# Scheduler priorities for weight loads, weight splits and accumulator readers in a two-layer decoder step

## The chip, the cores and the metric

The kernel runs on one core of one Trainium2 chip. The metric is device time in microseconds for one launch; the time before is the median of three runs, 2555.13 us (2554.44 to 2561.5).

## The reference

One inference step of a two-layer decoder over a prompt of 1024 tokens and 8 single-token samples that share all weights; model width 1024, feed-forward width 2816, all in float32.

```python
hn = rmsnorm(h, g[0])
mix = a_mixer(hn, ...) if l < N_A else b_mixer(hn, ...)   # one layer of each
h = h + rmsnorm(mix, g[1])
h = h + rmsnorm(swiglu(rmsnorm(h, g[2]), w_gu[l], w_down[l]), g[3])
# swiglu(x) = (silu(x @ gate) * (x @ up)) @ w_down
```

Mixer A is a gated linear recurrence (4 heads, a 128 x 128 state per head) beside cross-attention into 256 memory tokens. Mixer B is stick-breaking attention over one shared key and value projection, beside the same kind of memory attention. For the 8 samples the shared keys and values come from a paged cache and the memory keys and values from a cache of their own.

## The kernel before

**Tiling.** The tokens are cut into two groups: group 0 has 512 prompt tokens, group 1 has 512 prompt tokens and the 8 samples (520 columns, done as two matmuls of 260). Activations lie feature by token. Float32 precision is made from fast matmuls: each operand is split into a rounded part and a remainder, and three products are summed (line 261). An activation is split by `split_to` (lines 270 to 272).

**A projection.** `proj` (lines 256 to 268) makes 128 output features: eight 128-row blocks of the weight, three products each, so 24 matmuls of 512 columns for group 0 and 48 of 260 for group 1, all summed in one accumulator tile `mm` (two such tiles exist, line 62). Its weight comes from `split_w` (lines 240 to 254), in two tiles of 4 blocks: SyncE issues the load of 256 KB into `raw` (tag `w`, 5 buffers, line 51), ScalarE makes the rounded part (line 250), VectorE the remainder (line 251), both in a `ws` tile (5 buffers, line 52). The buffers of both tags thus hold two and a half projections of eight blocks. `mem_values` (lines 598 to 618) uses the same two tags without `split_w`.

**Readers of the accumulators.** In the feed-forward block (class `ffn`, line 459, method `part`) the gate's accumulator is read by VectorE in `silu` (line 281), the up projection's by the multiplication at line 474, and the down projection's by `evac_raw` (lines 397 to 405): a ScalarE copy for the first part (line 401), a VectorE addition to the sum `r` after that (line 403). `silu` is also used by mixer A's query and gate projections, and `evac_raw` by the output projection (line 420).

**What sets the order.** The main function (lines 1143 to 1195) emits the stages and interleaves them by hand: `weave` takes turns between an attention or recurrence stage and the projections of another group. The framework then builds each engine's queue when the program is compiled: it steps through the program on its own clock, and whenever an engine is free it takes, of the instructions whose inputs and buffers are ready by that clock, the one with the lowest priority number, which is the order of emission. On the chip each engine runs its queue in that fixed order and waits on semaphores. The stages named below are the start (`start`, lines 329 to 366, which loads the tokens, squares them at line 322 and transposes them at line 352), the recurrence's sample step (`hgrn_sample`, line 816, with one-column matmuls at line 849), stick-breaking attention over the prompt (`sb_prompt`, lines 1032 to 1078, with the sums through line 1063 and the values at line 1075), and the attention of the samples (`sample_scores` and `sample_pv`, lines 671 to 714, with VectorE work of 1024 elements a partition at lines 690, 691 and 702).

Of the kernel before, what the change touches and what calls it, by code (L numbers as in the profile page):

```python
# [8 lines left out]
F32 = mybir.dt.float32  # L9
F32R = mybir.dt.float32r  # L10
# [3 lines left out]
ALU = mybir.AluOpType  # L14
# [3 lines left out]
P = 128  # L18
# [4 lines left out]
def tile_decoder(  # L23
# [6 lines left out]
    nc = tc.nc  # L30
# [16 lines left out]
    def pool(name, bufs, **kw):  # L47
        return ctx.enter_context(tc.tile_pool(name=name, bufs=bufs, **kw))

    const = pool("const", 1)  # L50
    wraw = pool("wraw", 5)
    wspl = pool("wspl", 5)
# [15 lines left out]
    def nm(s):  # L68
        uid[0] += 1
        return f"{s}_{uid[0]}"  # L70

    def T(dt=F32):
        return tpool.tile([P, WID], dt, tag="t", name=nm("t"))
# [13 lines left out]
    def M(dt=F32):  # L87
        return mpool.tile([P, 2, WID], dt, tag="m", name=nm("m"))
# [4 lines left out]
    def R_one():  # L93
        r = rpool.tile([P, ND, WID], F32, tag="r", name=nm("r"))
        return [r[:, k, :] for k in range(ND)]
# [11 lines left out]
    def small(shape, dt=F32, tag="sm", bufs=None):  # L107
        return spool.tile(shape, dt, tag=tag, name=nm(tag), bufs=bufs)
# [39 lines left out]
    for lv in range(7):  # L148
        m = 1 << lv
# [17 lines left out]
    def gcol(l, i, k):  # L167
        o = (l * 4 + i) * ND + k
        return par[:, o : o + 1]
# [64 lines left out]
    def pv(ps, g):  # L234
        return ps[:, 0, :G] if g == 0 else ps[:, :, : PW[1]]

    def sv(ap, g):
        return ap[:, :G] if g == 0 else ap.rearrange("p (a n) -> p a n", a=2)

    def split_w(W, k0, nk, m0):  # L240
        out = []
        for a in range(0, nk, 4):
            n = min(4, nk - a)
            raw = wraw.tile([P, 4, P], F32, tag="w", name=nm("w"))
            nc.sync.dma_start(
                raw[:, :n, :],
                W[(k0 + a) * P : (k0 + a + n) * P, m0 : m0 + P].rearrange("(k p) m -> p k m", p=P),
            )
            ws = wspl.tile([P, 2, 4, P], F32R, tag="ws", name=nm("ws"))
            nc.scalar.copy(ws[:, 0, :n, :], raw[:, :n, :])  # L250
            nc.vector.tensor_sub(ws[:, 1, :n, :], raw[:, :n, :], ws[:, 0, :n, :].bitcast(F32))  # L251
            for i in range(n):
                out.append((ws[:, 0, i, :], ws[:, 1, i, :]))
        return out

    def proj(g, W, k0, nk, m0, xt):
        w = split_w(W, k0, nk, m0)
        ps = mmp.tile([P, 2, 512], F32, tag="mm", name=nm("mm"))
        for k in range(nk):
            wh, wl = w[k]  # L260
            for wi, (wt, xi) in enumerate(((wh, 0), (wh, 1), (wl, 0))):
                for a in range(NPC[g]):
                    o = a * PW[g]
                    nc.tensor.matmul(  # L264
                        ps[:, a, : PW[g]], wt, xt[k][:, xi, o : o + PW[g]],
                        start=(k == 0 and wi == 0), stop=(k == nk - 1 and wi == 2),
                    )
        return ps

    def split_to(dst, src):  # L270
        nc.scalar.copy(dst[0], src)  # L271
        nc.vector.tensor_sub(dst[1], src, dst[0].bitcast(F32))  # L272

    def silu(dst, ps, g):


        n = NG[g]
        x = T()
        dst = T() if dst is None else dst
        d = dst[:, :n]  # L280
        nc.vector.tensor_scalar(sv(x, g), pv(ps, g), -44.0, None, op0=ALU.max)  # L281
        nc.scalar.activation(d, x[:, :n], AF.Exp, scale=-1.0)  # L282
        nc.scalar.activation(d, d, AF.Ln, bias=1.0)  # L283
        nc.scalar.activation(d, d, AF.Exp, scale=-1.0)  # L284
        nc.vector.tensor_mul(d, d, x[:, :n])  # L285
        return dst
# [11 lines left out]
    def sq_acc(acc, src, k, n):  # L298
        if k == 0:
            nc.scalar.activation(acc[:, :n], src, AF.Square)  # L300
        else:
            t = N()
            nc.scalar.activation(t[:, :n], src, AF.Square)  # L303
            nc.vector.tensor_add(acc[:, :n], acc[:, :n], t[:, :n])  # L304
# [92 lines left out]
    def evac_raw(g, R, ps, m, acc, first, last):  # L397
        n = NG[g]
        dst = sv(R[m], g)
        if first:  # L400
            nc.scalar.copy(dst, pv(ps, g))
        else:
            nc.vector.tensor_add(dst, dst, pv(ps, g))  # L403
        if last:
            sq_acc(acc, R[m][:, :n], m, n)

    class out_proj:
# [5 lines left out]
        def mm(self, xo, m0=0, m1=ND):  # L413
            g = self.g
            if m0 == 0:
                self.R = R_from(self.store)
                self.acc = small([P, WID], tag="st", bufs=3)
            for m in range(m0, m1):
                ps = proj(g, w_o[self.l], 0, ND, m * P, xo)
                evac_raw(g, self.R, ps, m, self.acc, True, True)  # L420
                yield
# [37 lines left out]
    class ffn:  # L459
# [4 lines left out]
        def part(self, pi):  # L464
            g, l = self.g, self.l
            n = NG[g]
            f0, nf = PARTS[pi]
            last = pi == len(PARTS) - 1
            mids = []
            for j in range(nf):  # L470
                pg = proj(g, w_gu[l], 0, ND, (f0 + j) * P, self.xt)
                sg = silu(None, pg, g)
                pu = proj(g, w_gu[l], 0, ND, DFF + (f0 + j) * P, self.xt)
                nc.vector.tensor_mul(sv(sg, g), sv(sg, g), pv(pu, g))  # L474
                mt = M(F32R)
                split_to((mt[:, 0, :n], mt[:, 1, :n]), sg[:, :n])
                mids.append(mt)
                yield
            if pi == 0:
                self.R = R_one()  # L480
            if last:
                self.acc = small([P, WID], tag="st", bufs=3)
            for m in range(ND):
                ps = proj(g, w_down[l], f0, nf, m * P, mids)
                evac_raw(g, self.R, ps, m, self.acc, pi == 0, last)
                if last and self.rows:
                    nc.scalar.activation(
                        self.R[m][:, :n], self.R[m][:, :n], AF.Copy, scale=gcol(l, 3, m)
                    )
                    if m == 3:  # L490
                        self.first_half()
                if m % 2:
                    yield
# [79 lines left out]
    def mem_keys(l):  # L573
        for h in range(H):
            w = split_w(w_mem_kv[l], 0, ND, h * P)
            pb = mmp.tile([P, 2, 512], F32, tag="mm", name=nm("mm"))
            ps, pt = pb[:, 0, :], pb[:, 1, :]
            for k in range(ND):
                wh, wl = w[k]
                for wi, (wt, xi) in enumerate(((wh, 0), (wh, 1), (wl, 0))):  # L580
                    nc.tensor.matmul(
                        ps[:, :NM], wt, memt[k // 2][:, xi, k % 2, :],
                        start=(k == 0 and wi == 0), stop=(k == ND - 1 and wi == 2),
                    )
            src = T()
            nc.scalar.copy(src[:, :NM], ps[:, :NM])
            nc.sync.dma_start(mks[l][:, h, :], src[:, :NM])
            for tb in range(2):
                nc.tensor.transpose(pt[:, tb * P : (tb + 1) * P], src[:, tb * P : (tb + 1) * P], ident)
            tok = T()  # L590
            nc.vector.tensor_copy(tok[:, :NM], pt[:, :NM])
            nc.sync.dma_start(
                mk_prompt[l, 0, :, h, :].rearrange("(t p) d -> p t d", p=P),
                tok[:, :NM].rearrange("p (t d) -> p t d", t=2),
            )
            yield
# [349 lines left out]
    class mixer_a:  # L946
# [6 lines left out]
        def fq(self):  # L953
            yield from gate_proj(self.g, self.W, self.xt, self.F, self.K)
            yield from heads2(self.g, self.W, 0, self.xt, silu, A, self.Q)
# [16 lines left out]
        def gate(self):  # L972
            yield from heads2(self.g, self.W, 12 * P, self.xt, silu, A, self.sg)
# [254 lines left out]
```

## Time and profile before

| | us |
|---|---|
| median of 3 runs (lowest, highest) | 2555.13 (2554.44, 2561.5) |
| profiled execution: its own time | 2559.18 |
| profiled execution: span of its instructions | 2557.5 |
| granted TensorE clock over the span | 0.992 |

The profile page is that of one execution. The busy time of an engine is the union of its instructions; matmuls overlap and their ends are modelled, so TensorE counts as busy when it runs slowly too. "PE" is TensorE's matmuls, "PEld" its weight loads, "DVE" VectorE, "ACT" ScalarE, "SPq" SyncE's queue, which issues nearly all DMAs. In a row of groups the numbers after the bar are busy us, mean ns of one, and the idle time before them with what ended it. A row of waits gives microseconds in total, times, and the longest. A row of stretches gives length, busy time of each engine with its count of instructions, the granted clock, and the DMA share and rate.

### The profile page before, as it was taken

How to read it: one execution, taken by the hardware profiler on the slowest of the kernel's cores; microseconds unless marked ns; L12 is line 12 of the kernel's file. 1: busy time of each engine (PE TensorE's matmuls, PEld its weight loads, DVE VectorE, ACT ScalarE, POOL GpSimd, SP SyncE). 2: the span in 40 equal slices, each digit the busy share in tenths (PEclk: the TensorE clock that was granted, in tenths of full speed). 3: DMA queues.
4: the chain of work that ended last, by engine and by line, in shares of the span. 5: the costliest groups of instructions: out<-in, count | busy, mean ns of one | idle time of the engine just before them, and what ended most of it. 6: DMA issues, size and time to landing. Idle time of an engine off the chain costs nothing.

```text
span 2557.5 us, 40523 instructions
## 1 busy us (share of the span) xinstructions
PE 2526.6 (99%) x15649; PEld 2205.3 (86%) x15649; DVE 1555.5 (61%) x2709; ACT 1183.6 (46%) x2186; POOL 40.7 (2%) x59
## 2 busy tenths in 40 slices
PE   8999999999999999999999999999999999999998
PEld 6888898888867888999999989867776798999998
DVE  6666566654675576555544576666678758444445
ACT  6346543243434455555433454566543245443334
POOL 1000000000000000000000000000021000000000
PEclk9999999998999999999999999999999999999999
DMA  6352242233563445322333446322157544333332
GB/s 183 110 161 71 73 150 77 65 111 110 158 182 91 128 153 178 103 86 60 97 94 92 125 146 189 113 82 75 46 175 217 156 125 125 111 88 100 95 92 67
DMA packets 457708, 297.91 MB, mean 116 GB/s; under 512 B 17573, under 2 KB 422642, under 8 KB 457514
## 3 DMA queue, kind: packets, MB, share of 16 engines
q1 hardware_dynamic: 454954, 286.92, 37.4%
q0 software_dynamic: 2560, 8.39, 1.1%
q8 instruction: 123, 2.02, 0.3%
q14 instruction: 71, 0.58, 0.1%
HBM read 265.44 MB, written 29.80 MB: 115 GB/s over the span
## 4 chain that ended last, share of the span: by engine, by line
issue 25%; PE 22%; DVE 1%; POOL 1%; DMA 1%; ACT 0%; DVEq 0%; POOLq 0%; SPq 0%; ACTq 0%
PE mm L264 21%; POOL c L731 1%; PE s L704 0%; DMA w<-in_w_gu 0%; DMA b<-qd 0%; DMA c<-in_cache_sb_v,pidx 0%; PE s L1125 0%; DVE c L690 0%; DVE sc L691 0%; PE ns L293 0%; PE s L440 0%; DVE yT L542 0%; DVE c L702 0%; PE s L508 0%; DVE yT L539 0%
## 5 line engine op out<-in xcount | busy, mean ns | idle before, releaser
L264 PE MATMUL mm<-x,ws 128*128 128x260 f32 (+1 forms) x10080 | 1676.5, 324 | 6.0 <-DVE ws L251 3.1
L264 PEld LDWEIGHTS mm<-x,ws 128*128 128x128 f32 x10080 | 1452.6, 189 | 167.4 <-issue 24.6
L250 ACT CAST ws<-w 128x512 fp32r<-128x512 f32 (+1 forms) x800 | 475.6, 595 | 911.9 <-PE mm L264 816.7
L251 DVE TENSOR_TENSOR ws<-w,ws 128x512 fp32r<-128x512 f32 (+1 forms) x800 | 522.2, 658 | 346.6 <-ACT ws L250 336.7
L264 PE MATMUL mm<-m,ws 128*128 128x260 f32 (+1 forms) x3168 | 542.6, 325 | 1.1 <-DVE t L474 0.5
L264 PEld LDWEIGHTS mm<-m,ws 128*128 128x128 f32 x3168 | 453.4, 188 | 59.8 <-issue 15.3
L403 DVE TENSOR_TENSOR r<-r,mm 128x520 f32<-128x520 f32 (+1 forms) x128 | 88.3, 690 | 88.9 <-PE mm L264 87.8
L281 DVE TENSOR_SCALAR t<-mm 128x512 f32<-128x512 f32 (+1 forms) x104 | 72.2, 694 | 110.2 <-PE mm L264 109.0
L474 DVE TENSOR_TENSOR t<-t,mm 128x512 f32<-128x512 f32 (+1 forms) x88 | 60.8, 691 | 116.1 <-PE mm L264 116.0
L285 DVE TENSOR_TENSOR t<-t,t 128x512 f32<-128x512 f32 (+1 forms) x88 | 61.1, 695 | 84.9 <-ACT t L284 84.8
L304 DVE TENSOR_TENSOR st<-st,n 128x512 f32<-128x512 f32 (+1 forms) x98 | 67.1, 691 | 6.9 <-ACT n L303 5.0
L272 DVE TENSOR_TENSOR m<-t,m 128x512 fp32r<-128x512 f32 (+1 forms) x88 | 61.0, 693 | 3.5 <-ACT m L271 1.6
L282 ACT ACTIVATE t<-t 128x512 f32<-128x512 f32 (+1 forms) x88 | 55.9, 635 | 12.1 <-DVE t L281 4.6
L271 ACT CAST m<-t 128x512 fp32r<-128x512 f32 (+1 forms) x88 | 54.9, 623 | 13.9 <-DVE t L474 6.9
L283 ACT ACTIVATE t<-t 128x512 f32<-128x512 f32 (+1 forms) x88 | 55.9, 635 | 2.6
L284 ACT ACTIVATE t<-t 128x512 f32<-128x512 f32 (+1 forms) x88 | 55.9, 635 | 2.3
L892 PEld LDWEIGHTS s<-a,a 128*128 128x128 f32 x448 | 53.4, 192 | 1.2
L892 PE MATMUL s<-a,a 128*128 128x64 f32 x448 | 53.1, 271 | 0.0
L731 POOL DMA_INDIRECT c<-in_cache_sb_k,pidx x16 | 16.6, 1038 | 1874.7 <-DVE r L403 1247.9
L1027 DVE SCALAR_TENSOR_TENSOR b<-b,b 128x512 f32<-128x512 f32 (+3 forms) x48 | 26.8, 558 | 29.7 <-ACT b L1026 29.3
L643 ACT ACTIVATE b<-s,nmx 128x256 f32<-128x256 f32 x64 | 29.8, 470 | 28.7 <-DVE nmx L637 28.7
L1075 PE MATMUL s<-b,a 128*128 128x512 f32 (+3 forms) x96 | 41.5, 514 | 0.3
(293 smaller groups left out, 1948.0 us busy)
## 6 DMA issues: line engine op xcount, KB each, us to landing
w<-in_w_gu SPq DMA_DIRECT2D x352, 256.0 KB
w<-in_w_down SPq DMA_DIRECT2D x160, 256.0 KB
w<-in_w_in_a SPq DMA_DIRECT2D x80, 256.0 KB
w<-in_w_o SPq DMA_DIRECT2D x64, 256.0 KB
w<-in_w_mem_kv SPq DMA_DIRECT2D x32, 256.0 KB
c<-in_cache_mem_k SPq DMA_DIRECT2D x16, 512.0 KB
c<-in_cache_mem_v SPq DMA_DIRECT2D x16, 512.0 KB
w<-in_w_kv SPq DMA_DIRECT2D x32, 256.0 KB
```

Source lines behind the costliest of these rows:

```text
L250: nc.scalar.copy(ws[:, 0, :n, :], raw[:, :n, :])
L251: nc.vector.tensor_sub(ws[:, 1, :n, :], raw[:, :n, :], ws[:, 0, :n, :].bitcast(F32))
L264: nc.tensor.matmul(ps[:, a, : PW[g]], wt, xt[k][:, xi, o : o + PW[g]], start=(k == 0 and wi == 0), stop=(k == nk - 1 and wi == 2),)
L272: nc.vector.tensor_sub(dst[1], src, dst[0].bitcast(F32))
L281: nc.vector.tensor_scalar(sv(x, g), pv(ps, g), -44.0, None, op0=ALU.max)
L282: nc.scalar.activation(d, x[:, :n], AF.Exp, scale=-1.0)
L283: nc.scalar.activation(d, d, AF.Ln, bias=1.0)
L285: nc.vector.tensor_mul(d, d, x[:, :n])
L304: nc.vector.tensor_add(acc[:, :n], acc[:, :n], t[:, :n])
L403: nc.vector.tensor_add(dst, dst, pv(ps, g))
L474: nc.vector.tensor_mul(sv(sg, g), sv(sg, g), pv(pu, g))
L892: nc.tensor.matmul(plv[:, hh, c, :], K_[:, hh, cs], rhs, start=True, stop=True)
```

## The change

Three places are put under `tc.high_priority(offset=N)`, which lowers the priority number of the instructions in the block by N, as if they had been emitted N instructions earlier. The arithmetic, tiles, buffers and the sequence of emission stay the same.

```diff
     def split_w(W, k0, nk, m0):
         out = []
-        for a in range(0, nk, 4):
+        with tc.high_priority(offset=400):
+            for a in range(0, nk, 4):
...             # load, cast and remainder as before, one level deeper
     def silu(dst, ps, g):
...
-        nc.vector.tensor_scalar(sv(x, g), pv(ps, g), -44.0, None, op0=ALU.max)
+        with tc.high_priority(offset=100):
+            nc.vector.tensor_scalar(sv(x, g), pv(ps, g), -44.0, None, op0=ALU.max)
     def evac_raw(g, R, ps, m, acc, first, last):
...
+        with tc.high_priority(offset=100):
+            if first:
+                nc.scalar.copy(dst, pv(ps, g))
+            else:
+                nc.vector.tensor_add(dst, dst, pv(ps, g))
     # ffn.part
...
-                nc.vector.tensor_mul(sv(sg, g), sv(sg, g), pv(pu, g))
+                with tc.high_priority(offset=100):
+                    nc.vector.tensor_mul(sv(sg, g), sv(sg, g), pv(pu, g))
```

More of the change, by code (lines that the diff above doesn't have):

```diff
@@ L241, in split_w @@
         out = []
-        for a in range(0, nk, 4):
[L243 to L253, printed above, removed]
+        with tc.high_priority(offset=400):
+            for a in range(0, nk, 4):
+                n = min(4, nk - a)
+                raw = wraw.tile([P, 4, P], F32, tag="w", name=nm("w"))
+                nc.sync.dma_start(
+                    raw[:, :n, :],
+                    W[(k0 + a) * P : (k0 + a + n) * P, m0 : m0 + P].rearrange("(k p) m -> p k m", p=P),
+                )
+                ws = wspl.tile([P, 2, 4, P], F32R, tag="ws", name=nm("ws"))
+                nc.scalar.copy(ws[:, 0, :n, :], raw[:, :n, :])
+                nc.vector.tensor_sub(ws[:, 1, :n, :], raw[:, :n, :], ws[:, 0, :n, :].bitcast(F32))
+                for i in range(n):
+                    out.append((ws[:, 0, i, :], ws[:, 1, i, :]))
         return out
@@ L399, in evac_raw @@
         dst = sv(R[m], g)
[L400 to L403, printed above, removed]
+        with tc.high_priority(offset=100):
[3 more added lines that the diff above has]
+                nc.vector.tensor_add(dst, dst, pv(ps, g))
         if last:
```

## The prediction

> **What bounds the kernel.** I read the page first: the span and the engines' busy time.
>
> ```profile
> span 2557.5 us, 40523 instructions
> ...
> PE 2526.6 (99%) x15649; PEld 2205.3 (86%) x15649; DVE 1555.5 (61%) x2709; ACT 1183.6 (46%) x2186; POOL 40.7 (2%) x59
> ```
>
> TensorE is busy for all but 30.9 us of the span, and the change takes no matmul away. What can be won is therefore that idle time and time in which TensorE runs below its clock. Next, the page's groups for the instructions that are moved, and the waits of ScalarE and of SyncE's queue in front of them:
>
> ```profile
> L264 PE MATMUL mm<-x,ws 128*128 128x260 f32 (+1 forms) x10080 | 1676.5, 324 | 6.0 <-DVE ws L251 3.1
> ...
> L250 ACT CAST ws<-w 128x512 fp32r<-128x512 f32 (+1 forms) x800 | 475.6, 595 | 911.9 <-PE mm L264 816.7
> L251 DVE TENSOR_TENSOR ws<-w,ws 128x512 fp32r<-128x512 f32 (+1 forms) x800 | 522.2, 658 | 346.6 <-ACT ws L250 336.7
> ```
>
> ```profile
> SPq L245 <- DVE ws L251: 1643.8, 692, 13.3
> ```
>
> ```profile
> ACT ws L250 <- PE mm L264: 816.7, 502, 7.4
> ```
>
> There are 800 loads, 800 casts and 800 remainders. Before 692 of the loads SyncE stood waiting for a remainder to give a raw buffer back, and before 502 of the casts ScalarE stood waiting for TensorE to give a `ws` buffer back. There the weights are as early as five buffers allow, and a lower priority number cannot bring them earlier. It can act only where a load, cast or remainder had its buffer and stood behind other work. To find that place I took the stretches in which TensorE is not full:
>
> ```profile
> 0.00:21.00 21.00, 10.98 (x34) 7.50 (x35) 11.41 (x32) 13.00 (x28) 7.29 (x27) 1.00 0.80 234
> ...
> 700.00:720.00 20.00, 18.59 (x79) 13.85 (x77) 18.76 (x26) 4.34 (x10) 0.00 (x0) 1.00 0.75 213
> 720.00:740.00 20.00, 18.97 (x75) 12.55 (x74) 18.22 (x25) 5.79 (x10) 0.00 (x0) 1.00 0.67 195
> 1900.00:1920.00 20.00, 18.18 (x72) 14.27 (x71) 18.66 (x25) 6.73 (x11) 8.69 (x10) 0.91 0.79 224
> ...
> 1980.00:2000.00 20.00, 16.97 (x67) 13.65 (x68) 16.45 (x22) 6.14 (x10) 0.00 (x0) 0.91 0.74 222
> 1880.00:2040.00 160.00, 153.94 (x637) 112.02 (x636) 131.40 (x185) 52.26 (x97) 27.95 (x27) 0.98 0.66 201
> ...
> 2120.00:2500.00 380.00, 379.94 (x3041) 372.04 (x3041) 194.37 (x301) 158.58 (x268) 0.00 (x0) 1.00 0.34 101
> ```
>
> The start has 10.0 us of idle TensorE, 700 to 740 has 2.4, 1880 to 2040 has 6.1. A pure feed-forward stretch (2120 to 2500) is full to 0.06 us: nothing is to be won there. The middle two are the stages where the samples' attention runs beside the feed-forward block, and there VectorE is the crowded engine (18.76 of 20 us, 18.66 of 20). The groups of those stretches name what TensorE waited for, first 1895 to 1990, then 700 to 730:
>
> ```profile
> L264 PE MATMUL mm<-x,ws 128*128 128x512 f32 x234 | 57.7, 407 | 5.1 <-DVE ws L251 3.1 <-DVE t L474 1.8 <-ACT ws L250 0.3
> ```
>
> ```profile
> L264 PE MATMUL mm<-m,ws 128*128 128x512 f32 x96 | 23.7, 399 | 1.1 <-DVE t L474 0.5 <-DVE r L403 0.4 <-DVE ws L251 0.2
> ```
>
> All of it is remainders, casts and accumulator readers, the instructions that the change moves forward. The worst place in order of time:
>
> ```profile
> 1979.54 1.22 DVE L691 TENSOR_REDUCE sc<-c 128x8 f32<-128x1024 f32 x1
> 1980.67 0.68 DVE L474 TENSOR_TENSOR t<-t,mm 128x512 f32<-128x512 f32 x1
> ...
> 1981.26 1.22 DVE L691 TENSOR_REDUCE sc<-c 128x8 f32<-128x1024 f32 x1
> ...
> 1982.39 0.68 DVE L272 TENSOR_TENSOR m<-t,m 128x512 fp32r<-128x512 f32 x1
> 1982.99 2.49 DVE L251 TENSOR_TENSOR ws<-w,ws 128x512 fp32r<-128x512 f32 x4
> ```
>
> Four remainders ran in one go at 1982.99, behind sample reductions of 1.22 us; TensorE had nothing to multiply.
>
> **The change, part by part.** No instruction is added or removed; each term is a wait that goes or comes.
>
> *Remainders, casts and readers in the sample stages.* With the change they stand ahead of lines 690, 691 and 702 whenever both are ready; what runs already is finished first (at most 1.22 us), and the second accumulator and the `ws` buffers cover that. I take the whole of 5.1 + 1.1 = 6.2 us as gone. Bounds: 0, if the queues come out in another unlucky order, and 6.2.
>
> *The clock after those waits.* The granted clock fell right behind the wait above:
>
> ```profile
> 1983.70:1986.00 2.30, 2.27 (x5) 1.82 (x6) 2.30 (x4) 0.00 (x0) 0.00 (x0) 0.50 0.76 230
> ```
>
> The two 20 us stretches at 0.91 lost 2 x 20 x 0.09 = 3.6 us of full-speed work. If the waits go, this goes: -3.6 (bounds -3.6 and 0). [...]
>
> *What the samples pay.* Their VectorE work is now last in line. 1880 to 2040 leaves VectorE 28.6 of 160 us idle, which can hold it; the output projection that follows needs their result. Bounds 0 and 6.2 (all that was won is waited for again); I take +2.0, near the wait that exists already:
>
> ```profile
> PE s L704 <- DVE c L703: 1.9, 2, 1.0
> ```
>
> *The start.* The first projection is emitted well within 400 instructions of the program's beginning, so its five loads now have the lowest numbers of all and need nothing but free buffers. Before, in order of time:
>
> ```profile
> 0.79 0.40 SPq L120 DMA_DIRECT2D xtok<-in_x_prompt  x1
> 1.25 0.57 SPq L114 DMA_DIRECT2D prow<-in_g_norm  x1
> ...
> 3.03 1.30 SPq L120 DMA_DIRECT2D xtok<-in_x_prompt  x3
> ...
> 4.70 1.06 ACT L322 ACTIVATE c<-xtok 128x1024 f32<-128x1024 f32 x1 [2.63 <-DMA xtok<-in_x_prompt]
> ...
> 9.12 1.04 ACT L322 ACTIVATE c<-xtok 128x1024 f32<-128x1024 f32 x1
> ...
> 10.72 1.04 ACT L322 ACTIVATE c<-xtok 128x1024 f32<-128x1024 f32 x1
> ...
> 15.19 0.80 PE L264 MATMUL mm<-x,ws 128*128 128x512 f32 x1 [0.81 <-ACT x L355]
> ```
>
> Five weight issues (about 0.4 us each, as the token's 0.40) and the four small ones from 1.25 to 3.03 come before the first token load: it is issued at 0.79 + 2.0 + 1.8 = 4.6 instead of 0.79, so the first squares begin near 8.4 instead of 4.70. At their own pace of 1.6 us (9.12 to 10.72) the fourth begins at 8.4 + 4.8 = 13.2, 2.5 later; the weights' casts, now done by then, give a few tenths back. I take +2.2. Bounds: -0.8 (nothing is late and the wait of 0.8 at 15.19 goes) and +5.6 (1.31 MB of weights go through first at the 234 GB/s of the first 21 us).
>
> *Everywhere else* (attention over the prompt, normalisations): within 2.5 projections the order shifts by one or two instructions of 0.6 to 0.7 us; I take 0, with the slower rival's price as the bound above.
>
> Sum: -6.2 - 3.6 + 2.0 + 2.2 = **-5.6 us**. The profiled execution took 2559.18 (1.7 us outside its span of 2557.5) and would take 2553.6. It is 4.05 above the median, so the forecast on the median is 2555.13 - 5.6 = **2549.5 us**.
>
> **Rivals.**
>
> *More is won* (2541.5). The clock is down elsewhere too, beside the one-column matmuls of the recurrence's sample step:
>
> ```profile
> 560.00:567.00 7.00, 7.00 (x23) 5.79 (x22) 1.39 (x2) 0.62 (x1) 0.00 (x0) 0.52 0.50 147
> ...
> 584.00:591.00 7.00, 7.00 (x23) 5.74 (x22) 0.69 (x1) 0.62 (x1) 0.00 (x0) 0.52 0.44 144
> ...
> 611.00:622.00 11.00, 11.00 (x56) 11.00 (x56) 1.34 (x3) 0.49 (x2) 0.00 (x0) 0.53 0.42 128
> ```
>
> That cost 7 x 0.48 x 2 + 11 x 0.47 = 11.9 us. If ready weights let the queue put dense products between the thin ones, half of it goes (-6), and the samples' 2.0 is not paid: 2549.5 - 8.0 = 2541.5. Against it: TensorE was not waiting there (11.00 of 11 busy), so weights were no obstacle.
>
> *The change does little* (2557). The counts of 692 and 502 speak for it: the buffers set the pace, the waits in the sample stages come back in another form, and only the start's 2.2 is felt.
>
> *Slower, by stick-breaking attention* (2568). A block's two accumulations at line 1063 wait for a cast and a subtraction on ScalarE and VectorE:
>
> ```profile
> L1063 PE MATMUL s<-b,trir 128*128 128x512 f32 (+3 forms) x96 | 38.9, 408 | 1.4 <-ACT b L271 0.8
> ```
>
> ```profile
> PEld s L1063 <- ACT b L271: 10.3, 34, 0.7
> ```
>
> Of 96 blocks, 34 already see their weight load wait 0.30 us. If a weight's cast (0.60) or remainder (0.66) now stands in front of that cast on the chip, TensorE, whose order is fixed, waits with the feed-forward's products behind it. If the other 62 wait as long, that is +18.6: 2568. It ends slower by over 0.3% once it eats 13.3 us, some 44 of the 62. [...] Against the rival: the queue is built with such delays in view, and only 1.4 us of idle TensorE stand before these 96.
>
> **How the numbers follow.** Forecast 0.43, with a range of its own from 2543 to 2556; more won 0.19; little 0.15; slower 0.23. About 0.3% (7.7 us) is what a measurement of this kernel can tell from no change: faster is below 2547.5, slower above 2562.8. A third of the forecast's case (0.14) and the first rival make faster 0.33; the slower rival nearly alone makes slower 0.22; the rest is 0.45. The range reaches from 2536, just past the first rival, to the slower rival's 2568, where about half of that case is left out.
>
> **What would show it.** Right: no idle before line 264 by lines 251, 474 and 403 in the two sample stages, a granted clock of 1.00 there, weight loads first in SyncE's queue and the first product of line 264 near 17.4 us. Wrong: waits of line 264 for lines 251 or 474 as long as before (the first term); the first product at 15 us (the start); waits at lines 704 or at the output projection's first products over 5 us (the samples); more idle before lines 1063 and 1075 (the last rival); or a clock below 1.00 in stretches where it is full now.

## The result and the profile after

| | before | after |
|---|---|---|
| median us (lowest, highest; runs) | 2557.58 (2553.58, 2563.02; 7) | 2568.92 (2565.26, 2571.46; 7) |
| ratio of the two, 95% interval | | 1.0049 [1.0038, 1.0061] |
| profiled execution, span | 2557.5 | 2567.2 |
| granted clock over that span | 0.992 | 0.995 |

The changed kernel is 0.49% slower where 0.2% faster was forecast, and ends 0.9 us above the range. The lines of the kernel stand 1 to 4 further down: line 251 is now 252 (remainder), 264 is 265 (product), 474 is 478, 1063 is 1067. The page of the changed kernel, the span, the engines and the two rows of products (from the tokens `x`, and from the feed-forward's inner product `m`):

```profile
span 2567.2 us, 40625 instructions
...
PE 2521.9 (98%) x15649; PEld 2198.1 (86%) x15649; DVE 1560.0 (61%) x2706; ACT 1186.4 (46%) x2189; POOL 50.6 (2%) x59
...
L265 PE MATMUL mm<-x,ws 128*128 128x260 f32 (+1 forms) x10080 | 1668.0, 323 | 2.9 <-DVE x L273 1.5
...
L265 PE MATMUL mm<-m,ws 128*128 128x260 f32 (+1 forms) x3168 | 544.6, 326 | 4.3 <-DVE t L478 2.0
```

The second of these rows before:

```profile
L264 PE MATMUL mm<-m,ws 128*128 128x260 f32 (+1 forms) x3168 | 542.6, 325 | 1.1 <-DVE t L474 0.5
```

TensorE is busy for 4.7 us less (2521.9 instead of 2526.6) in a span that is 9.7 longer: it is idle for 45.3 us instead of 30.9, 14.4 more. The first row's idle time fell from 6.0 to 2.9, but the second's rose from 1.1 to 4.3, so the products wait for 7.2 us where they waited for 7.1. What they wait for has changed: the waits for remainders (3.3 us in all) are gone, those for accumulator readers only fell from 2.6 to 2.0 (line 478, once), and 4.8 us for splits of tokens and of `m` are new. The rest of the new idle time is elsewhere.

To place it I summed TensorE's matmul work along each trace (each matmul counted by its shape) and asked at which time both traces had done the same amount. The difference of the two times is the lag of the changed kernel; only the stretches where it moved are listed:

```text
stretch (us, before)              lag gained   lag then
start, to the first products           +9.1       +9.1
76 to 138                              +1.5      +10.2
586 to 655, recurrence sample step     -5.5       +4.1
717 to 784, first sample stage         -1.4       +2.5
913 to 975, first key/value proj.      +3.3       +6.6
1484 to 1546, second key/value proj.   +3.9      +10.6
1889 to 2090, second sample stage      -1.1       +9.8
all others (each within 0.8)           -          +10.0 at the end
```

Two kinds of place lose: the start, and the two places where a normalisation feeds the key and value projection. The timeline of the changed kernel's first 25 us, to be laid beside that of before:

```profile
0.79 9.99 SPq L246 DMA_DIRECT2D w<-in_w_in_a  x10
...
10.83 0.57 SPq L114 DMA_DIRECT2D prow<-in_g_norm  x1
...
12.61 1.78 SPq L120 DMA_DIRECT2D xtok<-in_x_prompt  x4
...
14.51 0.45 PE L164 MATMUL s<-ident,prow 128*128 128x128 f32 x1 [14.51 <-DMA prow<-in_hg_lb]
...
16.20 1.06 ACT L324 ACTIVATE c<-xtok 128x1024 f32<-128x1024 f32 x1 [0.51 <-DMA xtok<-in_x_prompt]
...
21.08 1.04 ACT L324 ACTIVATE c<-xtok 128x1024 f32<-128x1024 f32 x1
...
24.90 1.22 PE L265 MATMUL mm<-x,ws 128*128 128x512 f32 x2
```

Ten weight loads, not five, stand ahead of everything in SyncE's queue, and they hold it for 9.99 us. The first token load is issued at 12.61 instead of 0.79, the first square runs at 16.20 instead of 4.70, the first product at 24.90 instead of 15.19. What held the queue is in SyncE's waits over the first 13 us:

```profile
SPq L246 <- DVE ws L252: 3.6, 4, 1.3
SPq L246 <- DMA w<-in_w_in_a: 1.2, 2, 0.7
...
SPq L246 <- DVE cmpr L135: 0.7, 1, 0.7
```

There are five raw buffers. Loads six to ten wait for VectorE to give one back: four waits are named after a remainder, and one after the small mask instruction that ran just behind the fifth remainder. The tokens' load stands behind them in the same queue. The row of loads ends at ten because only five remainders run ahead of the first product: their five `ws` buffers come back behind products. At the normalisations, the stretches of 50 us with the two key/value projections (length, busy PE, PEld, DVE, ACT, POOL with counts, clock, DMA share, GB/s), of before and then of after:

```profile
900.00:950.00 50.00, 49.96 (x335) 44.91 (x335) 43.12 (x69) 27.85 (x49) 0.00 (x0) 1.00 0.49 151
...
1500.00:1550.00 50.00, 49.90 (x371) 46.63 (x372) 32.10 (x54) 20.65 (x37) 0.00 (x0) 1.00 0.46 140
```

```profile
900.00:950.00 50.00, 48.00 (x333) 42.80 (x332) 43.83 (x69) 27.67 (x48) 0.00 (x0) 1.00 0.41 129
...
1500.00:1550.00 50.00, 46.69 (x313) 41.65 (x313) 34.41 (x57) 22.19 (x39) 0.00 (x0) 1.00 0.44 133
```

TensorE was full there before (0.04 and 0.10 us idle), and now misses 2.0 and 3.3 us; what it waits for are the splits of the normalised tokens and the copies behind the first products (the groups of 1500 to 1550, after):

```profile
L265 PE MATMUL mm<-x,ws 128*128 128x260 f32 (+1 forms) x293 | 45.1, 310 | 2.0 <-DVE x L273 1.0 <-ACT x L272 1.0
L1008 PE MATMUL s<-ident,t 128*128 128x128 f32 x16 | 2.6, 283 | 1.2 <-ACT t L1003 1.2
```

### The profile page after: what moved, and what is told of

Read it like the earlier page. It is cut to its first block, busy times and chain, and to the rows that moved or that the text cites. A ratio compares the mean times of both kernels' runs of the same rounds, so it can differ in the third digit from the quotient of the medians.

```text
span 2567.2 us, 40625 instructions
## 1 busy us (share of the span) xinstructions
PE 2521.9 (98%) x15649; PEld 2198.1 (86%) x15649; DVE 1560.0 (61%) x2706; ACT 1186.4 (46%) x2189; POOL 50.6 (2%) x59
## 4 chain that ended last, share of the span: by engine, by line
PE 67%; issue 26%; DVE 3%; ACT 2%; DMA 1%; POOL 1%; SPq 0%; DVEq 0%; POOLq 0%; ACTq 0%
PE mm L265 56%; PE s L896 2%; POOL c L735 1%; PE s L667 1%; PE mm L612 1%; PE mm L585 1%; PE s L636 1%; PE s L708 1%; DVE ws L252 1%; PE s L660 1%; PE s L1067 0%; PE s L1079 0%; ACT ws L251 0%; PE ns L295 0%; PE s L923 0%
## 5 line engine op out<-in xcount | busy, mean ns | idle before, releaser
L735 POOL DMA_INDIRECT c<-in_cache_sb_k,pidx x16 | 23.1, 1445 | 1878.2 <-DVE r L406 1244.3
```

## The experiments

Each was run in up to 12 executions beside the kernel before on the same chip. One thing has to be separated first. Executions of one and the same kernel spread over some 10 us, and the spread follows the granted clock of the execution: of the 24 runs of the kernel before that stand beside head_spared, the spans at a clock of 0.991 and 0.992 are 2559.2 to 2560.2, those at 0.995 and 0.996 are 2550.3 to 2552.4. A thousandth of clock over 2556 us is 2.6 us; a line fitted over the 186 executions of this table, each taken from the mean of its own kernel and chip, gives 2.3. The last two columns split each difference of the means that way: what the mean clock explains (at 2.6), and the rest, which is work that came later or earlier. The standard error of a difference of means is about 1 us (1.7 for held_sample), so a rest below 1 can't be told from none.

| kernel | ratio to before [95%] | mean clock, this and before | by the clock, us | the rest, us |
|---|---|---|---|---|
| head_spared | 1.0011 [1.0002, 1.0020] | 0.9949, 0.9937 | -3.1 | +5.1 |
| five_first | 1.0030 [1.0018, 1.0042] | 0.9932, 0.9937 | +1.4 | +5.9 |
| ten_first | 1.0049 [1.0036, 1.0062] | 0.9938, 0.9937 | -0.2 | +12.3 |
| readers_only | 0.9996 [0.9986, 1.0007] | 0.9939, 0.9937 | -0.5 | -0.2 |
| norm_first | 1.0021 [1.0010, 1.0031] | 0.9952, 0.9940 | -3.3 | +9.2 |
| norm_alone | 1.0034 [1.0021, 1.0048] | 0.9935, 0.9940 | +1.2 | +7.2 |
| sample_alone | 0.9985 [0.9975, 0.9994] | 0.9953, 0.9940 | -3.3 | -0.7 |
| sample_readers | 0.9966 [0.9954, 0.9979] | 0.9955, 0.9940 | -3.9 | -4.3 |
| held_norm | 0.9999 [0.9989, 1.0008] | 0.9934, 0.9932 | -0.4 | +0.4 |
| held_only | 0.9995 [0.9986, 1.0004] | 0.9933, 0.9932 | -0.1 | -0.8 |
| held_head | 0.9979 [0.9970, 0.9988] | 0.9953, 0.9932 | -5.3 | +0.3 |
| held_sample | 0.9957 [0.9944, 0.9970] | 0.9952, 0.9932 | -5.0 | -3.8 |

**The start.** Theory: the weight loads ahead of the tokens cost about 9 us. Three kernels: the change without weights ahead of the first projection's own place (the offset grows from 0 to 400 as the program goes on), and the kernel before with only the first five, and only the first ten, weight tiles moved.

```diff
 # head_spared, on the changed kernel; wp[0] is the last weight tile's place
-        with tc.high_priority(offset=400):
+        with tc.high_priority(offset=woff()):   # max(0, min(400, p - wp[0] - 10))
 # five_first (5) and ten_first (10), on the kernel before
+            with tc.high_priority(offset=400 if wn[0] <= 5 else 0):
```

> The changed kernel, with the weights' offset cut at the start so that no weight comes ahead of the first projection's place; from there it grows with the distance to 400. Theory A (the start): the first product of the projections came at 24.90 us instead of 15.19, and this is the loss. Then the first product is back at 15 to 16 us, and the time falls by 9 to 10, to within 3 us of the kernel before (2557.6). Theory B (crowding: casts and remainders stand in front of other work on ScalarE and VectorE, as the prediction's slower rival had it): the time stays at 2564 or more.

> The kernel before, with only the first five weight tiles (load, cast, remainder) 400 ahead; nothing else is moved. The prediction's arithmetic for the start (five loads ahead of the tokens) gives +2.2 to 2.5 us and the first product near 17.5. Theory A, that it was ten loads, says the same of five. The rival, that the weights' bytes and not the order of issue delay the tokens, says +5.6 and a first product near 21.

> The kernel before, with only the first ten weight tiles 400 ahead. Theory A (five more loads wait for the first five remainders and hold SyncE's queue until then): first token load issued near 12.6 us, first product near 25, +9 to 10 us in all. Theory B: +2 to 6, since the rest of the kernel is as before.

head_spared's median is 2559.11 against 2556.68, and its first product runs at 15.35; the lag at the start is +0.2 instead of +9.1. ten_first alone has +8.8 at the start, its first token load goes out at 12.01 and its first product runs at 24.75, and its median is 2568.05: the loss of the start comes from ten tiles. With five, the lag at the start is +4.9. The timeline of five_first:

```profile
0.79 2.65 SPq L249 DMA_DIRECT2D w<-in_w_in_a  x5
...
5.42 3.30 SPq L120 DMA_DIRECT2D xtok<-in_x_prompt  x4
...
12.10 0.20 ACT L180 ACTIVATE lbt<-lbt 128x4 f32<-128x4 f32 x1 [2.38 <-DVE lbt L179]
12.21 1.04 ACT L326 ACTIVATE c<-xtok 128x1024 f32<-128x1024 f32 x1
...
20.80 1.22 PE L268 MATMUL mm<-x,ws 128*128 128x512 f32 x2
```

The issues took 2.65 us for five (0.53 each) and the tokens' load went out at 5.42, near the 4.6 of the prediction. But the first square ran at 12.21 instead of the 8.4 of the prediction. Its last visible wait is no transfer: a small exponential (line 180) stands in front of it on ScalarE and waits 2.38 us for VectorE, which was busy with weight remainders (the last at 9.05) and with masks. When the tokens were there can't be read from this trace. The first product at 20.80 and the +4.9 are near the rival's numbers (21 and +5.6, by the weights' bytes), not near those of the prediction's arithmetic. The DMA engines were busy for 0.98 of 3.5 to 8 us and 0.90 of 8 to 12, so bytes can't be ruled out. Of the five tiles' cost the issues are some 0.5 us each; how much of the rest is bytes and how much is the queue order on ScalarE and VectorE stays open.

**The readers.** The kernel before with lines 281, 401, 403 and 474 100 ahead and no weight moved.

```diff
 # readers_only, on the changed kernel
-        with tc.high_priority(offset=400):
+        with tc.high_priority(offset=0):
```

> The changed kernel with the weights' offset set to 0: only the accumulators' readers are 100 ahead. Theory A: the start is as before (first product at 15.2) and the time is within 4 us of before; the waits at the two normalisations near 940 and 1530 us (3.3 and 3.9 us later in the changed kernel) do not appear, because they are the casts' doing. Theory B with the readers as its cause: these waits are there, +5 to 7 us.

2556.16 against 2556.68, ratio 0.9996 [0.9986, 1.0007]: by themselves the readers change nothing that can be measured, and the lag has no step at the normalisations. Both losses belong to the weights.

**The normalisations.** First, are the steps the weights' doing in that place? norm_alone moves weights only from the first product of the output projection to the end of each key/value projection. norm_first takes head_spared and puts the scalings and splits of `normed`, and the copies of line 999 behind the key/value products, 500 ahead of their place, so that weights no longer pass them.

```diff
 # norm_alone, on the kernel before: offset 400 between these lines, else 0
+    OFF[0] = 400
     drain(o1.mm(a1.xo, 0, 1))
...
     drain(kv_proj(0, xk0))
+    OFF[0] = 0
 # norm_first, on head_spared (normed)
+            with tc.high_priority(offset=500):
                 t = N() if keep else R[k]
```

> The kernel before, with the weights 400 ahead only in the two stretches from the first product of the output projection up to the end of the key and value projection; readers not moved. Theory A: +7 us, in two steps of 3 to 4 us near 940 and 1530 us; TensorE waits there for the normalisation's split (lines 271, 272) and for line 999. Rival (the steps need the other moves too): within 2 us of before.

> The changed kernel with the start spared as in head_spared, and with two more things 500 ahead: the normalisation's own scaling and split (lines 310 to 312 of the kernel before) and the copy that reads the key and value projection's accumulator (line 999). Theory A (at the two normalisations, near 940 and 1530 us, casts of weights that still wait for a buffer stand in front of this work on ScalarE): the two steps of 3.3 and 3.9 us go, and the time is 6 to 7 us below head_spared, near 2552.5, faster than before by 0.1 to 0.2%. Rival (it is the order on TensorE itself, in which two projections are interleaved as their inputs arrive, that costs the time): the steps stay, 2559.

norm_alone has the two steps, +3.2 and +4.5, and is slower by 0.34%. norm_first did not take them away (+4.0 and +3.3, and some +1.7 more behind the first). That speaks against the theory that weights' casts pass the normalisation's own work on ScalarE, but doesn't settle it, since this edit moved other work too, as comes out below. What VectorE did while the key/value projection waited told more. The groups on VectorE from the first scaling of this normalisation to the last split, in the kernel before (922.6 to 938.9), then in norm_alone (913.8 to 932.5):

```profile
L310 DVE SCALAR_TENSOR_TENSOR n<-r,par,st 128x512 f32<-128x512 f32 x8 | 5.8, 746 | 1.5 <-ACT st L295 1.4
L272 DVE TENSOR_TENSOR x<-n,x 128x512 fp32r<-128x512 f32 x8 | 5.3, 684 | 0.0
L251 DVE TENSOR_TENSOR ws<-w,ws 128x512 fp32r<-128x512 f32 x5 | 3.4, 684 | 0.0
L310 DVE SCALAR_TENSOR_TENSOR r<-r,par,st 128x512 f32<-128x512 f32 x3 | 2.2, 747 | 0.0
```

```profile
L325 DVE SCALAR_TENSOR_TENSOR n<-r,par,st 128x512 f32<-128x512 f32 x8 | 5.8, 746 | 1.5 <-ACT st L310 1.5
L286 DVE TENSOR_TENSOR x<-n,x 128x512 fp32r<-128x512 f32 x8 | 5.3, 684 | 0.0
L325 DVE SCALAR_TENSOR_TENSOR r<-r,par,st 128x512 f32<-128x512 f32 x7 | 5.1, 747 | 0.0
L265 DVE TENSOR_TENSOR ws<-w,ws 128x512 fp32r<-128x512 f32 x5 | 3.4, 684 | 0.0
```

The remainders are five in both. What is new is the row `r<-r`: seven instead of three. These are the scalings of the *second* normalisation of the same sum (`xb0`, emitted after the key/value projection, so with a far higher priority number). No priority holds them back: whenever VectorE has nothing else ready by the clock of the framework's scheduler, they are taken, and in the fixed queue they then stand in front of a split that comes ready a moment later. In the changed kernel, in order of time:

```profile
942.55 1.41 DVE L312 SCALAR_TENSOR_TENSOR r<-r,par,st 128x512 f32<-128x512 f32 x2
942.66 0.62 ACT L272 CAST x<-n 128x512 fp32r<-128x512 f32 x1 [1.85 <-DVE n L312]
943.88 0.68 DVE L273 TENSOR_TENSOR x<-n,x 128x512 fp32r<-128x512 f32 x1
```

The cast that the last split needs is done at 943.28; the split itself starts at 943.88, behind two scalings. That there are more such moments with the weights moved is read from the counts; why the scheduler sees more of them isn't shown. norm_first put these scalings 500 ahead too, since both normalisations use the same lines, and had eight of them in front.

Theory "scalings" against rival "weights" (the rounding and the remainders themselves make the chain late) was tested by making the second normalisation depend on the last split of the first, with eight VectorE instructions on one column each. The values don't change (gain plus 0 times a remainder).

```diff
 # held_norm on norm_alone, held_only on the kernel before,
 # held_head on head_spared, held_sample on sample_readers
+    gs0 = after_split(xk0, 1, 0)       # gg[:, k] = 0 * last split + gcol(1, 0, k)
     drain(kv_proj(0, xk0))
-    weave((normed(0, f0.R, f0.r, lambda k: gcol(1, 0, k), xb0), 8), ...
+    weave((normed(0, f0.R, f0.r, gs0, xb0), 8), ...
```

> norm_alone (the kernel before, weights 400 ahead only from the first output projection to the end of each key/value projection), with the second normalisation's scalings made to depend on the last split of the first: its eight gain columns are copied into a small tile (gain + 0 x that remainder), eight tiny VectorE instructions. Nothing is left out. Theory 'scalings': in norm_alone 7 or 8 in-place scalings of the second normalisation (0.74 us each) stand on VectorE among the 8 scalings and splits that the key/value projection waits for, against 3 before; held back, the stretch from first residual sum to last split falls from 44 us to 41 or less, PE's idle time there to under 0.5, both steps of the drift (+3.2, +4.5) go to under 1, and the time is within 0.1% of before (ratio 0.999 to 1.001). Rival 'weights': the rounding and remainders themselves, taken earlier, make the chain late; the steps stay at +2 to +4 each and the ratio at 1.002 to 1.0035.

> The kernel before, only with the second normalisation's scalings held back as in held_norm; no priority is moved. Both theories: PE's idle time in the two normalisations was 0.0 and 0.07 us before, so nothing can be won there: ratio 0.999 to 1.001. A rise would be the price of the eight tiny instructions and of the later second normalisation, to be taken off held_norm's.

> head_spared (the change with no weight ahead of the first projection's place), with the second normalisation's scalings held back. Theory 'scalings': head_spared's 2559.1 less the two steps of 3.3 and 3.9, so 2552, ratio about 0.9985. Rival 'weights': 2559, ratio 1.001 to 1.002, with both steps in the drift.

held_norm's groups on VectorE in the same place (918.0 to 933.1):

```profile
L333 DVE SCALAR_TENSOR_TENSOR n<-r,par,st 128x512 f32<-128x512 f32 x8 | 5.8, 749 | 1.6 <-ACT st L310 1.5
L286 DVE TENSOR_TENSOR x<-n,x 128x512 fp32r<-128x512 f32 x8 | 5.4, 688 | 0.7 <-ACT x L285 0.7
L265 DVE TENSOR_TENSOR ws<-w,ws 128x512 fp32r<-128x512 f32 x4 | 2.7, 686 | 0.0
```

The `r<-r` row is gone. In its place VectorE idles 0.7 us for a cast, where the scalings had put 5.1 us. The stretch is 15.0 us long instead of 18.6, and the lag's steps fell from +3.2 and +4.5 to +0.4 and -0.1. The time is 0.9999 of before [0.9989, 1.0008] where norm_alone had 1.0034 [1.0021, 1.0048]. held_only, the price of the device by itself, is 0.9995 [0.9986, 1.0004]. held_head is 2551.86, where "scalings" expected 2552 and "weights" 2559; that it meets 2552 so well is in part luck, since only 4.8 us of its distance to head_spared are in the table's last column and 2.2 are clock. Its steps are +0.5 and +1.2 where head_spared has +3.3 and +3.9. Rival "weights" falls as the main cause; the +1.2 that is left in held_head stays without a cause. The rival stated for norm_first, the order on TensorE itself, forecast what norm_first measured (2559, here 2559.71). But norm_alone and held_norm, with and without the steps, have the same order of matmuls by tile and shape in all but 22 of 15649 places, so that order is hardly the cause. The number of scalings in front roughly orders the steps:

| kernel, normalisation | `r<-r` ahead of the last split | stretch, us | step of the lag, us |
|---|---|---|---|
| held_norm, first and second | 0, 0 | 15.0, 15.7 | +0.4, -0.1 |
| held_head, first and second | 0, 0 | 16.1, 16.8 | +0.5, +1.2 |
| before, first and second | 3, 3 | 16.2, 16.2 | 0 (the measure) |
| five_first and ten_first, second | 5, 5 | 17.4, 17.4 | +1.6, +1.6 |
| after, first | 7 | 18.6 | +3.3 |
| after, second | 8 | 19.5 | +3.9 |
| norm_alone, first and second | 7, 8 | 18.6, 19.6 | +3.2, +4.5 |
| norm_first, first and second | 8, 8 | 20.0, 19.6 | +4.0, +3.3 |

From zero to three nothing is lost by them, since TensorE still had the output projection's products to do; beyond three each costs it 0.7 to 0.9 us (3.2 and 3.3 for four more, 3.3 to 4.5 for five), near the 0.75 that one takes. The rows of five_first and ten_first, which moved nothing near that place, show how far a change of order at the start travels through the scheduler.

**The sample stages.** Weights 400 ahead only in the two stages where the samples' attention runs beside the feed-forward block, without and with the readers' 100, and the latter with the second normalisation held.

```diff
 # sample_alone and sample_readers, on the kernel before (both sample stages so)
+    OFF[0] = 400
     weave((chain(a1.merge(), a1.mem_sample(), a1.mem()), 32), (chain(f0.part(2), f0.part(3)), 16))
+    OFF[0] = 0
 # sample_readers besides: silu, evac_raw and the multiplication of ffn.part
+        with tc.high_priority(offset=100):
```

> The kernel before, with the weights 400 ahead only in the two stages where the samples' attention runs beside feed-forward parts 2 and 3; readers not moved. The prediction's first two terms: no wait of the projections for remainders there, the clock at 1.00, and 4 to 8 us less, of which 2 may be paid back at line 704. Rival (VectorE is full there, so another wait takes its place): within 2 us of before, with the projections waiting for a reader or a split instead.

> As sample_alone, with the accumulators' readers 100 ahead everywhere. If the readers' waits (lines 474, 403: 2.2 us in all before) are worth anything, 1 to 2 us less than sample_alone; the rival says no difference, as for the readers alone.

> sample_readers (the fastest so far: weights 400 ahead in the two sample stages alone, readers 100 ahead), with the second normalisation's scalings held back. Both theories: as sample_readers, 0.9955 to 0.9975 of before, since its normalisations have no step to lose; if it falls under 0.995, the three scalings that slip in before cost time too.

All three are faster than before: 0.9985, 0.9966 and 0.9957, with 2546.96 and 2547.17 us for the last two against 2554.53 and 2556.75 for before on their chips. The intervals of the last two overlap, so which of them is better isn't settled; both beat the kernel before and the changed one. The readers, which change nothing by themselves, take 4.3 us off the mean here (sample_readers against sample_alone on the same chip, standard error 1.2), more than the 1 to 2 expected. TensorE's idle time says the same: over 690 to 750 and 1880 to 2040 it is 8.5 us before, 7.6 in sample_alone and 4.0 in sample_readers, in line with the rest column's -0.7 and -4.3. The groups of TensorE from 1880 to 2040 in sample_readers:

```profile
L278 PE MATMUL mm<-x,ws 128*128 128x512 f32 (+1 forms) x441 | 91.0, 368 | 0.0
L278 PE MATMUL mm<-m,ws 128*128 128x512 f32 x192 | 50.9, 410 | 0.5 <-DVE m L286 0.4
L721 PE MATMUL s<-c,sel 128*8 128x512 f32 x32 | 16.9, 622 | 1.9 <-DVE c L720 1.9
```

The products wait 0.5 us instead of 5.1, and the sums of line 721 (before: 704) 1.9 instead of 0.9. In the first sample stage the products wait 1.6 us instead of 1.1, once, for a reader.

## Why the prediction was wrong

The sum of -5.6 was wrong in sign through two of its steps; the steps that gave the gain were right in kind, and came only in part.

- ***The start* is the step that failed most.** It read "its five loads now have the lowest numbers of all and need nothing but free buffers", and costed five issues: +2.2, bound +5.6. It measured +9.1 in the changed kernel and +8.8 alone. The second half of that sentence held the error: five is the number of raw buffers (the first projection has only two loads), and remainders run early too and give buffers back, so the loads of the next projections, also within the first 400 instructions, follow at once. Ten loads went ahead, five of them waiting for a buffer, with the tokens behind them in one queue. The first product came at 24.90, not 17.4. Even for five tiles the step was too low (+4.9, near its upper bound): the squares were reckoned from SyncE's issues alone (its terms give 8.5, not 8.4), while ScalarE had a small instruction in front that waited for VectorE, and the weights' bytes were on their way first. The prediction looked in the attention for work that stands behind another instruction of its engine; it was to be seen here (the square at 12.21 behind line 180's wait of 2.38 us) and at the normalisations (the split at 943.88, its cast done at 943.28).
- ***Everywhere else*, taken as 0, is the second.** It cost +3.3 and +3.9 at the two normalisations. The prediction weighed moved weights against the work that they pass; the loss came from work that was not moved at all and filled a gap of the scheduler. held_norm shows that holding this work back takes the steps away.
- ***Remainders, casts and readers in the sample stages* with *what the samples pay*.** -6.2 + 2.0 was forecast. In the changed kernel 2.5 us came (-1.4 and -1.1 of lag), since new waits took the place of the old. Its groups of TensorE from 1895 to 2045:

```profile
L265 PE MATMUL mm<-x,ws 128*128 128x512 f32 x349 | 80.0, 390 | 0.0
L265 PE MATMUL mm<-m,ws 128*128 128x512 f32 x182 | 49.8, 421 | 2.3 <-ACT m L272 1.9 <-DVE m L273 0.4
L708 PE MATMUL s<-c,sel 128*8 128x512 f32 x32 | 16.6, 614 | 2.0 <-DVE c L707 2.0
```

  The 5.1 us for remainders and readers went to 0.0 as forecast; 2.3 came back as the splits of the feed-forward's own product, which are moved by neither offset, and 2.0 at the samples' sums (0.9 before). In the first sample stage the 1.1 us did not go but became 2.0: TensorE waits until 709.17 for the multiplication of line 478, which runs at 708.34 behind a sample reduction of 1.22 us and a remainder of 0.68. The step's words that "the second accumulator and the `ws` buffers cover that" failed there. In sample_readers, without the other parts, the rest column has -4.3, near the forecast's -4.2 of these two terms, but with another split: the products wait 4.1 us less, not 6.2, and the sums no longer than before (1.9).
- ***The clock after those waits*, -3.6, was right in kind and size where the start was left alone, and came only in part in the changed kernel.** Over 1880 to 2040 the granted clock is 0.96 to 0.98 in the profiles of the seven kernels that move no weights there (before among them), each with two dips; with weights ahead there it is 1.00 in head_spared, norm_first, sample_alone, held_head and held_sample, and 0.99 in sample_readers (one dip). The changed kernel still has 0.98, with two dips of 3.4 us at 1936.9 and 1960.8: they lie right behind the two new waits, of 1.39 us for a split's cast (until 1934.91) and of 1.96 us at the samples' sums (until 1960.20). Over many executions the six kernels with weights ahead in the sample stages and nothing at the start have mean clocks of 0.9949 to 0.9955, while their runs of before have 0.9932 to 0.9940: 3.1 to 5.3 us. The kernels that leave the sample stages alone stay at 0.9932 to 0.9939, and the seven executions of the changed kernel have 0.9944. Which waits bring a dip isn't settled: sample_alone waits 3.2 us at the sums and has none.
- **The lag's -5.5 at the recurrence's sample step is not the change's.** held_only has the same order of instructions on TensorE, VectorE and ScalarE as before up to the first of the two normalisations, and yet this stretch of it, where before had 0.53, runs at full clock:

```profile
611.00:622.00 11.00, 11.00 (x80) 10.39 (x80) 3.37 (x7) 3.34 (x7) 0.00 (x0) 1.00 0.61 183
```

  So the changed kernel's profile flatters it there. With the recurrence's -5.5 left out, the profiled lag of 10.0 would be 15.5. The medians differ by 11.3; the changed kernel's mean clock would make 1 to 3 us of the gap, and the rest of it isn't accounted for.
- **The rivals.** *More is won* did not come: between 530 and 640 the clock still falls two to four times in every one of the traces. *Slower, by stick-breaking attention* named a time near the measured one (2568) by a mechanism that did not act. The waits of its weight load after the change, where 34 waits of 10.3 us in all stood before:

```profile
PEld s L1067 <- ACT b L272: 10.3, 34, 0.7
```

  The count, the sum and the longest are the same, and the lag doesn't move by more than 0.4 in any stretch of those stages. *The change does little* was right that buffers set the pace nearly everywhere: the pure feed-forward stretch has a lag change of 0.0.

Left open: the +1.5 at 76 to 138 (head_spared has +1.4 there too), the +1.2 in held_head, and the split of five_first's start between bytes and queue order.

## What to carry to other kernels

A priority only orders what is ready; it doesn't hold anything back. Before raising one, count at the start how many of the raised transfers can go in a row as their buffers come free, because what stands behind them in their queue waits for the whole row (here ten loads, 9.99 us); and look for unrelated ready work that will fall into the gaps in front of a chain, which needs a dependence, not a priority, to stay behind. Raise it only in the stages whose waits name the raised instruction: 400 for the weights in two stages, with the readers' 100, took 0.34% off; 400 everywhere put 0.49% on.

## What the runs showed of the hardware

- The granted clock fell to half (0.50) in dips of 3.4, 6.8 and 10.2 us within the span, all multiples of one length. Within one trace all its falls and rises lie on one grid of 3.41 us (to 0.03 us), and the grid starts elsewhere in each trace (0.55 us after the span's start in before, 1.50 in after). With the same order of instructions before it one execution had the dip at 611 (before, 0.53 over 611 to 622) and one had not (held_only, 1.00). The dips came behind partly and fully busy stretches of TensorE alike: in the 3.4 us ahead of the dips at 1905.2 and 1983.7 (before) TensorE was busy for 1.58 and 0.70 us, and in those ahead of the dips at 560.3 and 584.2, with thin one-column matmuls among the products, for all 3.40. What share of work keeps the clock up isn't shown.
- Executions of one kernel, whose queues are the same each time, spread over 10 us: 2552.01 to 2561.97 us over 24 runs of the kernel before, with clocks of 0.996 to 0.991. For effects of 5 us, the mean clock of many executions is a better witness than any one trace.
- Five 256 KB loads were issued in 2.65 us when buffers were free (five_first), and ten took 9.99 us where the second five had to wait for buffers to come back (after).
